# A hybrid decoder layer on one core: 16 more tokens by gathered expert rows, a dense stage on 336 instead of 352, and other queues and pacing

## Chip, core and metric

The kernel runs on one core of a Trainium2 chip. The metric is the device time of one execution in microseconds; the kernel before was timed three times. One execution was also profiled; the numbers below are from it.

## The reference

For 512 tokens of width 2048 the layer does two things, in fp32:

```
h = rms_norm(x);  proj = h @ w_in
y_a = causal attention, 16 latent heads (q, k, v from low-rank projections, rotary part)
y_b = causal attention, 16 heads with forget gates
x  = x + (concat(y_a, y_b) * sigmoid(gates)) @ w_out            # out projection, 4096 x 2048
h2 = rms_norm(x);  q = h2 @ w_q                                 # 8 heads x 2 x 128
s1, s2 = q . sub_keys (128 keys each); top 16 of each; the 256 sums; top 16 of these
e  = i1 * 128 + i2 (of 16384 experts);  g = softmax of the 16 scores
out = x + sum over the 128 picks of a token: g * gelu(h2 . u[e]) * v[e]
```

Each token so picks 8 heads x 16 = 128 experts, and each expert has a row of 2048 floats (8 KB) in u and one in v.

## The kernel before

All large products are done as three fp32r matmuls on a high and a low part of each operand (`mm3`, L131). Every weight arrives in pieces of 128 x 1024 floats (512 KB, `load`, L94, on SP's queue), which are cut in two *halves*; for each half ACT casts a high part (`half_hi`, L105) and DVE subtracts it for the low part (`half_lo`, L110). Raw pieces rotate through 3 buffers, and 2 (in the output projection) or 1 (in the dense stage) spare ones from `spare` (L602), which lie in memory that an earlier phase has used.

The order of each engine's work is set at build time: a planner simulates the program and puts each engine's instructions in the order in which it finds them ready; each engine and each queue then works in that order. Pools hand out buffers, and a new tile waits for the last reader of what lay there.

**Phase 1** (0 to about 1476 us) does the projections and attention of all heads. Each head's gated output is written to `mrg` in memory (L315, on SP).

**Phase 2** (to 1924 us) is the output projection. `out0_units` (L679) does tokens 0 to 127 first, so that their experts are known early: `bring(q)` loads the merged heads of those tokens in four blocks (three on SP, one on POOL) and splits them, then 96 *early* halves (blocks 0 to 2) and 32 *late* ones (block 3) follow. The 128 *main* units (L575, `out_units`) do tokens 128 to 511 with 9 matmuls of 512 columns a half; they read `merged_half` (L631), four loads of 192 KB on ACT's queue. Six main units stand between the norm of tokens 0 to 127 and their query, 8 among the query's halves, the others after it. `select` (L793) then gives the picks of tokens 0 to 127 in `idx`.

From there on the *gathers* run beside the matmuls. One gather (`gather`, L911) is an indirect DMA on POOL that brings, for one pick of 128 tokens, 128 rows of 8 KB (1.05 MB) into one of three row buffers `rows`, and one DVE operation on 128 x 2048 floats: a dot product with h2 for u (L927), a multiply-add for v (L940). `half_lo` adds `rate` to a credit for each half and issues a gather for each whole credit (L112). In phase 2 the rate is `RATE` = 0.42 after a start of -`LAG` x `RATE`; in the dense stage it is what is left over `HALVES` = 948. There are `GATHERS` = 2 x (128 + 32): after the first 128 tokens, 32 further ones (`NX`) are gathered with four picks side by side: partition 32 j + t holds token t and the picks of block j. Their indices and gates are moved to that layout by small DMAs on ACT's queue (L906), `h0` is filled with four copies of their h2 (L932), and at the end a matmul with a 0/1 matrix `C_RM` adds the four blocks up (L975).

**Phase 3** (to about 2179 us) scales x to h2 for tokens 128 to 511 (L860), transposes and splits it (L867), does the query on 384 columns, top-k and select. The first r of the dense stage (`ahead`) are mixed in.

**Phase 4**, the dense stage, does the experts for the remaining TD = 384 - 32 = 352 tokens without gathering: all 16384 experts, with zero gates for those not picked. `gate_matrix` (L979) builds the gates from the picks, four tokens at a time (a *group*: 3 + 1 DVE compares, 3 ACT scalings, 4 matmuls, one ACT copy). `up_stream` (L1026) computes u . h2 for 128 experts (one r) in 48 matmuls, `gated` (L1067) applies gelu and gate, and `down` (L1079) adds v's part in 48 matmuls per r. All of these have TD columns. `store` (L1100) transposes the sums back, adds x and writes.

Of the kernel before, what the change touches and what calls it, by code (L numbers as in the profile page):

```python
# [48 lines left out]
C_N = C_I2 + NKEY  # L49
# [3 lines left out]
NX = 32  # L53
NG = P // NX
# [11 lines left out]
RATE = 0.42  # L66
# [4 lines left out]
FIRST_W = {0: (0, 0), 2: (1, 0), 4: (0, 1), 6: (1, 1)}  # L71
WAIT = 6
# [6 lines left out]
class Kern:  # L79
    def __init__(self, tc, a):  # L80
        self.tc, self.nc, self.a = tc, tc.nc, a
        self.gathered, self.credit, self.rate = 0, 0.0, 0.0
        self.early = {}
        self.nraw, self.nbuf = -1, NRAW
# [182 lines left out]
    def attention(self, parts, fpart, v, gate, hx, yq=None):  # L267
# [47 lines left out]
        nc.sync.dma_start(self.mrg[hx % HEADS * 2 + hx // HEADS], gate)  # L315
# [241 lines left out]
    def phase2(self, res, sm):  # L557
# [12 lines left out]
        with self.pool(name="mgr", bufs=2) as self.mgr, self.pool(name="msp", bufs=3) as self.msp, \  # L570
# [6 lines left out]
            seq = self.out0_units(tk) + [norm] + main[:WAIT] + turns  # L577
            done = WAIT
# [16 lines left out]
            self.run(main[done:])  # L595
            self.rate = 0.0

# [33 lines left out]
    def merged_half(self, q, i):  # L631
# [47 lines left out]
    def out0_units(self, tk):  # L679
# [5 lines left out]
        def bring(q):  # L685
# [3 lines left out]
            eng = nc.gpsimd if q == 3 else nc.sync  # L689
            eng.dma_start(raw, self.mrg[q * 8:q * 8 + 8, :, 0:P].rearrange("h p t -> p h t"))  # L690
# [16 lines left out]
        def own():  # L707
# [134 lines left out]
    def phase3(self, hp):  # L842
# [7 lines left out]
        with self.pool(name="tk", bufs=2) as tk, \  # L850
# [55 lines left out]
            for j in range(NG):  # L906
                js, rows = slice(j * NX, j * NX + NX), slice(j * NX, j * NX + NX)
                nc.scalar.dma_start(self.idxx[rows], self.idx1[:NX, js])
                nc.scalar.dma_start(self.gx[rows], flat(self.gt[:, 0])[:, js])

    def gather(self, g):  # L911
        n = PH * TOPK
        if g < n:
            self.gather_u(g)
        elif g < 2 * n:
            self.gather_v(g - n)
        elif g < 2 * n + NX:
            self.extra_u(g - 2 * n)
        else:
            self.extra_v(g - 2 * n - NX)  # L920

    def gather_u(self, k):
        nc = self.nc
        row = self.rows[:, k % 3]
# [4 lines left out]
        if k == PH * TOPK - 1:  # L929
            nc.scalar.activation(self.aa, self.aa, AF.Gelu)  # L930
            nc.vector.tensor_tensor(out=self.aa, in0=self.aa, in1=self.gt0.rearrange("p a b -> p (a b)"), op=OP.mult)
            for j in range(NG):  # L932
                nc.gpsimd.dma_start(self.h0[j * NX:j * NX + NX], self.hx)

    def gather_v(self, k):
        nc = self.nc
        row = self.rows[:, k % 3]
# [7 lines left out]
    def extra_rows(self, src, s):  # L945
        row = self.rows[:, s % 3]
# [4 lines left out]
    def extra_u(self, s):  # L951
        nc = self.nc
        row = self.extra_rows("u", s)
        nc.vector.tensor_tensor_reduce(out=row, in0=row, in1=self.h0, scale=1.0, scalar=0.0,
                                       op0=OP.mult, op1=OP.add, accum_out=self.ax[:, s:s + 1])
        if s == NX - 1:
            nc.scalar.activation(self.ax, self.ax, AF.Gelu)
            nc.vector.tensor_tensor(out=self.ax, in0=self.ax, in1=self.gx, op=OP.mult)

    def extra_v(self, s):  # L960
        nc = self.nc
        row = self.extra_rows("v", s)
        sum_ = self.h0
        if s == 0:
            nc.vector.tensor_scalar(out=sum_, in0=row, scalar1=self.ax[:, 0:1], scalar2=None, op0=OP.mult)
        else:
            nc.vector.scalar_tensor_tensor(out=sum_, in0=row, scalar=self.ax[:, s:s + 1], in1=sum_,
                                           op0=OP.mult, op1=OP.add)
        if s == NX - 1:
            x = self.rows[:NX, (s + 1) % 3]  # L970
# [286 lines left out]
```

## Time and profile before

| | us |
|---|---|
| three runs, median (lowest, highest) | 4208.79 (4203.27, 4209.16) |
| the profiled execution | 4210.52 |
| its span, first to last instruction | 4208.7 |

| engine | busy us | share of the span |
|---|---|---|
| PE (matmul) | 4107.9 | 98% |
| PEld (weight load, beside PE) | 3716.1 | 88% |
| DVE | 3094.0 | 74% |
| ACT | 1919.4 | 46% |
| POOL | 593.0 | 14% |

Matmuls are pipelined, so the mean duration of one is longer than the distance from one to the next (its pitch); a pitch is read from the count of records in a stretch that PE fills. Engine names: PE TensorE, DVE VectorE, ACT ScalarE, POOL GpSimd, SP SyncE; a q behind a name is the engine's sequencer, which waits and issues DMAs. L12 is line 12 of the kernel. In a window's row the columns are the stretch, its length, then the busy time with the number of records for PE, PEld, DVE, ACT and POOL, the granted TensorE clock as a share of 2.4 GHz, the busy share of the 16 DMA engines, and GB/s. In a timeline's row they are the start, the time from the first start to the last end of the merged instructions, engine, line, operation, out<-in, form and count, and in brackets the idle time before with what ended it.

### The profile page before, as it was taken

To read this page: it belongs to the slowest core of one execution; us is meant where nothing else is said; L and a number is where in the kernel's file an instruction comes from. 1 tells how busy PE (TensorE), PEld (TensorE's weight loads), DVE (VectorE), ACT (ScalarE), POOL (GpSimd) and SP (SyncE) were. 2 spreads that over 40 slices of the span, in tenths; PEclk is the share of its full clock that TensorE was granted. 3 is DMA by queue.
4 is the path that set the end of the run, shared out by engine and by line. 5 is a ranking of instruction groups with operands and counts; after the bars stand their busy time and mean duration, and the time that the engine had idled before them with its cause. 6 is when DMAs were issued, how large, how long until landed. Compare 5 with 4: busy or idle time off the path is not lost.

```text
span 4208.7 us, 61121 instructions
## 1 busy us (share of the span) xinstructions
PE 4107.9 (98%) x22599; PEld 3716.1 (88%) x22599; DVE 3094.0 (74%) x5344; ACT 1919.4 (46%) x3708; POOL 593.0 (14%) x487
## 2 busy tenths in 40 slices
PE   8999999999999979998999999999999999999998
PEld 6878888888888757787999999999999999999998
DVE  8555555655565678887999887777777877777775
ACT  4555545555554566333369333333333333333332
POOL 1111101111111100021001111111211221211120
PEclk9999999999999989998999999999999999999999
DMA  3222222222222388797347988888888888888885
GB/s 133 88 74 83 80 81 83 83 74 88 85 76 83 117 288 269 268 346 267 111 136 225 339 300 312 308 308 318 312 305 300 318 303 314 317 311 308 297 302 195
DMA packets 246860, 905.20 MB, mean 215 GB/s; under 512 B 22977, under 2 KB 75201, under 8 KB 202049
## 3 DMA queue, kind: packets, MB, share of 16 engines
q1 hardware_dynamic: 192208, 547.82, 38.0%
q0 software_dynamic: 46704, 339.24, 21.8%
q10 hardware_dynamic: 7648, 14.25, 1.1%
q8 instruction: 177, 2.90, 0.3%
q14 instruction: 123, 1.00, 0.1%
HBM read 862.12 MB, written 39.06 MB: 214 GB/s over the span
## 4 chain that ended last, share of the span: by engine, by line
PE 44%; ACT 3%; DMA 1%; DVE 1%; issue 1%; POOL 0%; DVEq 0%; POOLq 0%; ACTq 0%
PE acc L136 8%; PE acc L135 8%; PE acc L134 8%; PE a L136 7%; PE a L135 7%; PE a L134 7%; ACT o L1005 2%; ACT rows L1019 1%; ACT whi L105 0%; DMA rows<-v,eidx 0%; DVE wlo L110 0%; DMA rows<-u,eidx 0%; DVE rows L927 0%; PE acc L1110 0%; PE acc L975 0%
## 5 line engine op out<-in xcount | busy, mean ns | idle before, releaser
L105 ACT CAST whi<-raw 128x512 fp32r<-128x512 f32 x1820 | 1120.9, 622 | 1835.6 <-PE acc L135 679.1
L110 DVE TENSOR_TENSOR wlo<-raw,whi 128x512 fp32r<-128x512 f32 x1820 | 1230.2, 688 | 642.6 <-ACT whi L105 615.7
L135 PE MATMUL acc<-Wl,whi 128*128 128x352 f32 x2048 | 660.7, 323 | 3.5 <-DVE Wl L92 3.5
L134 PE MATMUL acc<-Wh,whi 128*128 128x352 f32 x2048 | 655.7, 323 | 0.5 <-ACT Wh L91 0.5
L134 PE MATMUL a<-dh,whi 128*128 128x352 f32 x1984 | 640.7, 323 | 0.0
L135 PE MATMUL a<-dl,whi 128*128 128x352 f32 x1984 | 638.8, 322 | 0.0
L136 PE MATMUL a<-dh,wlo 128*128 128x352 f32 x1984 | 634.2, 322 | 1.7 <-DVE wlo L110 1.6
L136 PE MATMUL acc<-Wh,wlo 128*128 128x352 f32 x2048 | 627.0, 323 | 1.9 <-DVE wlo L110 1.9
L134 PE MATMUL mm<-hh,whi 128*128 128x512 f32 x1424 | 572.5, 402 | 8.3 <-ACT hh L536 8.3
L135 PE MATMUL mm<-hl,whi 128*128 128x512 f32 x1424 | 571.6, 402 | 6.2 <-DVE hl L537 6.0
L136 PE MATMUL mm<-hh,wlo 128*128 128x512 f32 x1424 | 569.8, 400 | 0.0
L135 PEld LDWEIGHTS acc<-Wl,whi 128*128 128x128 f32 x2048 | 385.4, 188 | 4.1 <-DVE Wl L92 4.1
L134 PEld LDWEIGHTS acc<-Wh,whi 128*128 128x128 f32 x2048 | 384.0, 188 | 1.8 <-issue 0.8
L136 PEld LDWEIGHTS acc<-Wh,wlo 128*128 128x128 f32 x2048 | 379.3, 188 | 3.1 <-DVE wlo L110 3.1
L136 PEld LDWEIGHTS a<-dh,wlo 128*128 128x128 f32 x1984 | 371.3, 188 | 2.9 <-DVE wlo L110 2.7
L135 PEld LDWEIGHTS a<-dl,whi 128*128 128x128 f32 x1984 | 372.4, 188 | 0.0
L134 PEld LDWEIGHTS a<-dh,whi 128*128 128x128 f32 x1984 | 372.4, 188 | 0.0
L135 PEld LDWEIGHTS mm<-hl,whi 128*128 128x128 f32 x1424 | 269.5, 189 | 72.3 <-DVE hl L537 11.1
L134 PEld LDWEIGHTS mm<-hh,whi 128*128 128x128 f32 x1424 | 270.2, 190 | 68.9 <-ACT hh L536 8.3
L136 PEld LDWEIGHTS mm<-hh,wlo 128*128 128x128 f32 x1424 | 269.6, 189 | 61.0 <-issue 0.2
L940 DVE SCALAR_TENSOR_TENSOR x<-rows,aa,x 128x2048 f32<-128x2048 f32 x128 | 300.1, 2345 | 2.2 <-DMA rows<-v,eidx 2.2
L927 DVE CUSTOM_DVE_ANT_0 rows<-rows,h 128x2048 f32<-128x2048 f32 x128 | 292.3, 2284 | 8.7 <-DMA rows<-u,eidx 8.7
(383 smaller groups left out, 6050.2 us busy)
## 6 DMA issues: line engine op xcount, KB each, us to landing
raw<-ut SPq DMA_DIRECT2D x256, 512.0 KB, 5.1
raw<-vt SPq DMA_DIRECT2D x256, 512.0 KB, 5.7
raw<-w_in SPq DMA_DIRECT2D x178, 512.0 KB, 3.7
raw<-w_out SPq DMA_DIRECT2D x128, 512.0 KB, 5.2
raw<-w_pq SPq DMA_DIRECT2D x64, 512.0 KB, 4.0
gd<-rows SPq DMA_DIRECT2D x22, 1024.0 KB, 5.8
G<-gd SPq DMA_DIRECT2D x15, 1408.0 KB, 8.0
raw<-w_up SPq DMA_DIRECT2D x24, 512.0 KB, 3.6
```

What stands on the lines that cost most here:

```text
L105: self.nc.scalar.copy(hi, src)
L110: ins = self.nc.vector.tensor_tensor(out=lo, in0=src, in1=hi.bitcast(F32), op=OP.subtract)
L134: nc.tensor.matmul(out, wh, xh, start=start, stop=False)
L135: nc.tensor.matmul(out, wh, xl, start=False, stop=False)
L136: nc.tensor.matmul(out, wl, xh, start=False, stop=stop)
L927: nc.vector.tensor_tensor_reduce(out=row, in0=row, in1=self.h0, scale=1.0, scalar=0.0, op0=OP.mult, op1=OP.add, accum_out=self.aa[:, k:k + 1])
L940: nc.vector.scalar_tensor_tensor(out=self.x1[0], in0=row, scalar=self.aa[:, k:k + 1], in1=self.x1[0], op0=OP.mult, op1=OP.add)
L1005: nc.scalar.activation(o1[:, i], o1[:, i], AF.Copy, scale=lists[:, 2, t0 + i:t0 + i + 1])
L1019: nc.scalar.copy(st[:, :, t4:t4 + 4], ps.rearrange("p t i -> p i t"))
```

## The change

- **Tokens.** 16 further tokens (`GROUPS` = (0, 32), (32, 16)) are gathered, with eight picks side by side. `NX` becomes 48, TD 336, `GATHERS` 352. The second group runs behind the first, with its own spread of h2 (8 copies), its own columns of indices and gates, and a 0/1 matrix `C_RB` for its reduction. The first group's sum now goes to `x1[0]`, whose store is done, so that `h0` is free for the second spread. Row buffers rotate by one counter (`next_row`).
- **Pacing.** `RATE` 0.46; the last `REST` = 10 main units of phase 2 give no credit.
- **Queues.** The gated output of the last two heads (hx 15 and 31) is written from POOL. All four `bring` loads go on POOL, the first three before any unit. `merged_half` loads its four heads by one DMA of 768 KB on SP into one buffer, behind a one-element DVE copy that waits for the last low part made (`load_after`), and splits two heads at a time.
- **Order.** `merged_half(0, 0)` comes after 64 early halves, `merged_half(0, 1)` after the first 8 late ones; `FEW` = 4 main units stand among the late halves, one behind each 8.
- **Buffers.** `w` in the dense stage, which `store` uses too, has four buffers instead of two.

```diff
+GROUPS = ((0, 32), (32, 16))
+NX = sum(n for _, n in GROUPS)
-RATE = 0.42
+RATE = 0.46
+REST = 10
+FEW = 4
@@ attention
-        nc.sync.dma_start(self.mrg[hx % HEADS * 2 + hx // HEADS], gate)
+        eng = nc.gpsimd if hx % HEADS == HEADS - 1 else nc.sync
+        eng.dma_start(self.mrg[hx % HEADS * 2 + hx // HEADS], gate)
@@ phase2
-            seq = self.out0_units(tk) + [norm] + main[:WAIT] + turns
-            done = WAIT
+            seq = self.out0_units(tk, main) + [norm] + main[FEW:FEW + WAIT] + turns
+            done = FEW + WAIT
...
-            self.run(main[done:])
+            self.run(main[done:-REST])
             self.rate = 0.0
+            self.run(main[-REST:])
@@ merged_half
-        for j in range(4):
-            m = self.mgr.tile([P, n], F32, name="m")
-            nc.scalar.dma_start(m, self.mrg[8 * q + 4 * i + j, :, t0:])
-            self.split(mh[:, j], ml[:, j], m)
+        m = self.mgr.tile([P, 4, n], F32, name="m")
+        k = 8 * q + 4 * i
+        self.load_after(m, self.mrg[k:k + 4, :, t0:].rearrange("h p t -> p h t"))
+        for j in (0, 2):
+            self.split(mh[:, j:j + 2], ml[:, j:j + 2], m[:, j:j + 2])
@@ out0_units
-            eng = nc.gpsimd if q == 3 else nc.sync
-            eng.dma_start(raw, self.mrg[q * 8:q * 8 + 8, :, 0:P].rearrange("h p t -> p h t"))
+            nc.gpsimd.dma_start(raw, self.mrg[q * 8:q * 8 + 8, :, 0:P].rearrange("h p t -> p h t"))
...
-        out = [self.bare(bring, q) for q in range(3)] + early[:48] + [self.bare(own)] + early[48:] + [self.bare(bring, 3)]
-        return out + late[:12] + [self.bare(self.merged_half, 0, 0)] + late[12:24] + \
-            [self.bare(self.merged_half, 0, 1)] + late[24:]
+        for q in range(3):
+            bring(q)
+        half = lambda i: [self.bare(self.merged_half, 0, i)]
+        out = early[:40] + [self.bare(own)] + early[40:64] + half(0) + early[64:] + [self.bare(bring, 3)]
+        for i in range(0, len(late), 8):
+            out += late[i:i + 8] + main[i // 8:i // 8 + 1] + (half(1) if i == 8 else [])
+        return out
@@ phase3
-            for j in range(NG):
-                js, rows = slice(j * NX, j * NX + NX), slice(j * NX, j * NX + NX)
-                nc.scalar.dma_start(self.idxx[rows], self.idx1[:NX, js])
-                nc.scalar.dma_start(self.gx[rows], flat(self.gt[:, 0])[:, js])
+            for o, n in GROUPS:
+                m = P * n // P
+                for j in range(P // n):
+                    js, rows = slice(j * m, j * m + m), slice(j * n, j * n + n)
+                    nc.scalar.dma_start(self.idxx[rows, o:o + m], self.idx1[o:o + n, js])
+                    nc.scalar.dma_start(self.gx[rows, o:o + m], flat(self.gt[:, 0])[o:o + n, js])
@@ gather
+    def spread(self, i):
+        o, n = GROUPS[i]
+        for j in range(P // n):
+            self.nc.gpsimd.dma_start(self.h0[j * n:j * n + n], self.hx[o:o + n])
+
+    def next_row(self):
+        self.nrow += 1
+        return self.rows[:, self.nrow % 3]
...
-        sum_ = self.h0
+        sum_ = self.x1[0] if i == 0 else self.h0
...
+            pick = C_RM if n == 32 else C_RB
             for c in range(4):
...
+                nc.tensor.matmul(ps[:n], self.cst[:, pick:pick + n], sum_[:, cs], start=True, stop=True)
@@ gated, store
-        w = self.wp.tile([P, 512], F32, name="w", bufs=2)[:, :TD]
+        w = self.wp.tile([P, 512], F32, name="w", bufs=4)[:, :TD]
```

## Rows read from the trace of the kernel before

**Rows 1.** The page: busy time by engine; the chain by engine.

```profile
PE 4107.9 (98%) x22599; PEld 3716.1 (88%) x22599; DVE 3094.0 (74%) x5344; ACT 1919.4 (46%) x3708; POOL 593.0 (14%) x487
...
PE 44%; ACT 3%; DMA 1%; DVE 1%; issue 1%; POOL 0%; DVEq 0%; POOLq 0%; ACTq 0%
```

**Rows 2.** Windows: stretch, length, PE PEld DVE ACT POOL busy (records), clock, DMA, GB/s.

```profile
1480.00:1620.00 140.00, 120.10 (x473) 87.23 (x474) 102.94 (x166) 90.94 (x164) 0.93 (x1) 0.93 0.84 288
1760.00:1780.00 20.00, 20.00 (x88) 16.16 (x87) 16.23 (x21) 6.22 (x10) 3.61 (x4) 1.00 1.00 402
1760.00:1900.00 140.00, 140.00 (x607) 113.36 (x606) 122.72 (x159) 49.63 (x91) 28.29 (x27) 1.00 0.93 353
1924.00:2000.00 76.00, 56.10 (x291) 51.83 (x291) 57.84 (x109) 23.18 (x49) 8.18 (x9) 0.82 0.67 258
2180.00:2310.00 130.00, 128.74 (x948) 123.62 (x947) 127.10 (x277) 130.00 (x372) 16.61 (x23) 1.00 0.74 210
2340.00:4140.00 1800.00, 1797.36 (x11216) 1795.62 (x11215) 1423.70 (x1803) 671.65 (x1174) 330.92 (x275) 1.00 0.85 309
```

**Rows 3.** Waits of PE: total us, times, longest.

```profile
PE pa L134 <- ACT whi L105: 12.7, 2, 12.5
PE tp L866 <- DVE dl L92: 12.5, 4, 7.0
```

**Rows 4.** Windows filled by matmuls of 256, of 352 and of 384 columns.

```profile
168.00:172.50 4.50, 4.50 (x39) 4.50 (x38) 3.14 (x6) 4.11 (x8) 0.00 (x0) 1.00 0.04 15
3000.00:3100.00 100.00, 100.00 (x625) 100.00 (x624) 79.47 (x93) 36.29 (x62) 20.03 (x15) 1.00 0.84 309
2001.00:2028.00 27.00, 27.00 (x157) 27.00 (x157) 26.97 (x134) 9.58 (x17) 0.00 (x0) 1.00 0.42 121
```

**Rows 5.** Groups by form, PE, one product of three: count, busy, mean ns, idle.

```profile
L134 PE MATMUL acc<-Wh,whi 128*128 128x352 f32 x2048 | 655.7, 323 | 0.5 <-ACT Wh L91 0.5
L134 PE MATMUL a<-dh,whi 128*128 128x352 f32 x1984 | 640.7, 323 | 0.0
...
L134 PE MATMUL acc<-dh,whi 128*128 128x352 f32 x64 | 20.8, 326 | 0.5 <-ACT whi L105 0.5
```

**Rows 6.** Timeline of DVE at the second border.

```profile
1932.49 2.29 DVE L927 CUSTOM_DVE_ANT_0 rows<-rows,h 128x2048 f32<-128x2048 f32 x1 [1.16 <-DMA rows<-u,eidx]
...
1938.22 2.29 DVE L927 CUSTOM_DVE_ANT_0 rows<-rows,h 128x2048 f32<-128x2048 f32 x1 [3.43 <-DMA rows<-u,eidx]
...
1979.10 2.28 DVE L927 CUSTOM_DVE_ANT_0 rows<-rows,h 128x2048 f32<-128x2048 f32 x1
```

**Rows 7.** The reduction's matmuls; the timeline of the tail.

```profile
L975 PE MATMUL acc<-h,cst x8: 593/593/617, 4144.6 to 4147.6; 128*32 128x512 f32 x8
...
4198.47 1.28 DVE L1111 TENSOR_TENSOR w<-w,acc 128x512 f32<-128x512 f32 x2 [0.57 <-PE acc L1110]
...
4201.71 0.33 ACTq L1107 DMA_DIRECT2D w<-xs  x1
4204.69 0.69 DVE L1111 TENSOR_TENSOR w<-w,acc 96x512 f32<-96x512 f32 x1 [4.93 <-DMA w<-xs]
```

**Rows 8.** Two lines' instructions: duration ns min/median/max, first and last start us.

```profile
L1018 PE MATMUL acc<-o,o x704: 270/275/378, 2179.1 to 2308.7; 128*128 128x128 f32 x176
...
L908 ACTq DMA_DIRECT2D idxx<-idx x4: 514/558/1432, 2172.4 to 2175.2; - x4
```

**Rows 9.** Timelines of ACT and of SP at the first border.

```profile
1484.98 0.51 ACT L91 CAST mh<-m 128x384 fp32r<-128x384 f32 x1 [6.18 <-DMA m<-mrg]
...
1459.20 17.63 SPq L315 DMA_DIRECT2D mrg<-gate  x2
...
1479.04 19.66 SPq L98 DMA_DIRECT2D raw<-w_out  x7
```

**Rows 10.** DMA issues: count, KB each, median us to landing.

```profile
raw<-mrg SPq DMA_DIRECT2D x3, 512.0 KB, 4.1
...
raw<-mrg POOLq DMA_DIRECT2D x1, 512.0 KB, 7.7
```

More of the change, by code (lines that the diff above doesn't have):

```diff
@@ L81, in __init__ @@
         self.tc, self.nc, self.a = tc, tc.nc, a
-        self.gathered, self.credit, self.rate = 0, 0.0, 0.0
+        self.gathered, self.credit, self.rate, self.nrow = 0, 0.0, 0.0, -1
         self.early = {}
@@ L569, in phase2 @@
         self.ss = sm.tile([P, NT, 4], F32, name="ss")
[L570 removed]
+        with self.pool(name="mgr", bufs=1) as self.mgr, self.pool(name="msp", bufs=3) as self.msp, \
                 self.pool(name="tka", bufs=1) as tk, self.spare(NRAW2, NSP2), \
@@ L677, in bare, with out0_units @@
         return lambda: None, lambda w: f(*v)
-    def out0_units(self, tk):
+    def out0_units(self, tk, main):
         nc, a = self.nc, self.a
@@ L916, in gather @@
             self.gather_v(g - n)
-        elif g < 2 * n + NX:
-            self.extra_u(g - 2 * n)
-        else:
-            self.extra_v(g - 2 * n - NX)
+        else:
+            g -= 2 * n
+            for i, (o, m) in enumerate(GROUPS):
+                if g < m:
+                    return self.extra_u(i, o, m, g)
+                if g < 2 * m:
+                    return self.extra_v(i, o, m, g - m)
+                g -= 2 * m
+    def spread(self, i):
[5 more added lines that the diff above has]
+        return self.rows[:, self.nrow % 3]
     def gather_u(self, k):
         nc = self.nc
-        row = self.rows[:, k % 3]
+        row = self.next_row()
         nc.gpsimd.indirect_dma_start(out=row, out_offset=None, in_=self.a["u"],
@@ L931, in gather_u @@
             nc.vector.tensor_tensor(out=self.aa, in0=self.aa, in1=self.gt0.rearrange("p a b -> p (a b)"), op=OP.mult)
-            for j in range(NG):
-                nc.gpsimd.dma_start(self.h0[j * NX:j * NX + NX], self.hx)
+            self.spread(0)
     def gather_v(self, k):
         nc = self.nc
-        row = self.rows[:, k % 3]
+        row = self.next_row()
         nc.gpsimd.indirect_dma_start(out=row, out_offset=None, in_=self.a["v"],
@@ L945, in extra_rows @@
     def extra_rows(self, src, s):
-        row = self.rows[:, s % 3]
+        row = self.next_row()
         self.nc.gpsimd.indirect_dma_start(out=row, out_offset=None, in_=self.a[src],
@@ L974, in extra_v @@
                 ps = self.acc.tile([P, 512], F32, name="acc")
-                nc.tensor.matmul(ps[:NX], self.cst[:, C_RM:C_RM + NX], sum_[:, cs], start=True, stop=True)
-                nc.vector.tensor_tensor(out=x[:, cs], in0=x[:, cs], in1=ps[:NX], op=OP.add)
-            nc.sync.dma_start(self.a["out"][P:P + NX], x)
+                nc.tensor.matmul(ps[:n], self.cst[:, pick:pick + n], sum_[:, cs], start=True, stop=True)
+                nc.vector.tensor_tensor(out=x[:, cs], in0=x[:, cs], in1=ps[:n], op=OP.add)
+            nc.sync.dma_start(self.a["out"][P + o:P + o + n], x)
     def gate_matrix(self, pool, acc, ahead):
@@ L1105, in store @@
             n = min(P, TD - q)
-            x = self.wp.tile([P, 512], F32, name="w", bufs=2)[:n]
+            x = self.wp.tile([P, 512], F32, name="w", bufs=4)[:n]
             nc.scalar.dma_start(x, self.xs[NX + q:NX + q + n, cs])
@@ L1179, in constants @@
         c[:, C_RM + h] = (p % 32 == h)
+    for h in range(16):
+        c[:, C_RB + h] = (p % 16 == h)
     c[:, C_IF] = (np.float32(10000.0) ** (-np.arange(32, dtype=np.float32) / np.float32(32)))[p % 32]
```

36 lines of the change are left out of this document (19 added, 17 removed).

## Prediction, made before the result was known

> **What bounds the kernel now.** I read the page's busy line and chain first, then busy time by stage, matmul pitch by width, TensorE's waits, and last the timelines at the stage borders. TensorE is busy 98% of the span and holds 44% of the chain; no other engine has more than 3% [rows 1]. By stage this is sharper: from 2340 to 4140 us, the dense expert stage, PE is busy 1797.4 of 1800 us at full granted clock with 11216 matmuls, while DMA moves 309 GB/s at share 0.85 and DVE is busy 79% [rows 2]. Nothing but the number of matmuls and the pitch of one sets that stage. What PE loses lies at the borders: 20 of 140 us from 1480 to 1620 at a mean clock of 0.93, and 20 of 76 us from 1924 to 2000 at 0.82 [rows 2]; its two largest waits are there, 12.7 us on a weight cast and 12.5 us on a split of the transposed h2 [rows 3].
>
> **The dense columns.** A matmul takes the time of its columns plus a constant: 100/625 = 160 ns at 352 columns, 27/157 = 172 ns at 384 and 4.5/38 = 118 ns at 256 [rows 4]; at 512 it is 140/607 = 231 ns [rows 2]. (A window counts a record at its edges, so the short ones are good to 3%.) The slopes are 0.38, 0.44 and 0.44 ns a column, so 16 columns fewer save 6.0 to 7.1 ns; I take 6.8, on the side of the longer windows. Three products each of 2048, 1984 and 64 matmuls run at this width [rows 5]: 12288 x 6.8 ns = 84 us (74 to 87). All of it is on the path, since PE has no other limit there; what is late next is a transfer or DVE, below.
>
> **The 32 more gathers.** Pacing gives 114 x 0.42 - 4.2 = 43 gathers in the output projection now and leaves 277 for the 948 halves of the dense stage, 0.292 a half. After: 100 x 0.46 - 4.6 = 41, and 311 left, 0.328 a half. A half is 12 matmuls, so the window holds 11216/12 = 935 halves and gets 34 more gathers: 35 MB at 1.05 MB each, and 34 x 2.3 us = 78 us of DVE [rows 6]. At the new pitch its 11216 matmuls take 11216 x 153.7 ns = 1724 us. DVE: (1424 + 78)/1724 = 87%; DMA: (556 + 35) MB/1724 us = 343 GB/s. The nearest row is the output projection, 1760 to 1900 us: 353 GB/s, DVE 122.7 of 140 us (88%), PE 140.00 of 140; for 20 us even 402 GB/s [rows 2]. So both loads have been carried beside a full PE, but for 140 us, not for 1700. Lower bound 0; upper, the rival below; I take +5 us for late landings, about twice the 2.6 us that PE idles in the stage today. The second group's reduction adds 4 fp32 matmuls, 8 records on PE: now 8 from 4144.6 to 4147.6 us [rows 7], so +3.5 us. The extra spreads of h and the row rotation hang on POOL, which is busy 331 of 1800 us [rows 2], and cost nothing unless a gather waits behind them: the second spread is issued 32 gathers before its use.
>
> **Gate matrix and index moves.** 88 groups become 84. The groups run from 2179.1 to 2308.7 us [rows 8], 1.47 us each, ACT 130.00 of 130 us busy [rows 2]: -5.9 us. Ahead of it ACT issues 12 index copies instead of 4, 0.56 us each [rows 8]: +4.5 us on the engine that is the limit. The 8 more gate copies are spread over the four query columns, where ACT is under half busy (49.6 of 140 us in the projection before it [rows 2]); 0. Net -1.5 us (-6 to +5).
>
> **First border, mixers to output projection.** PE stands until 1488.2 us for the first cast. ACT, in order, sat 6.18 us before a merged-heads piece until 1484.98, then cast the third block and only then the weights; SP sat behind the last gate's write for 17.63 us from 1459.2 and sent the next weight only at 1479.04 [rows 9]. Afterwards the merged halves can't come early (their load waits for a DVE copy behind a late weight), and the gate's write and the three blocks are POOL's. So both stalls go. Next late is the last gate itself: the two spare raw buffers lie where its tile lay (the 1479.04 load waited for that write), and the first weights now fall to them. With the write at about 1480, 4.5 us of flight and 0.6 us of cast I get 1485.5: -2.5 us. The four early main halves bring 9 matmuls of 231 ns each against some 0.9 us of DMA, and give back about 1.2 us each of the DMA-bound stretch: -5 us. Against it, 1.5 MB of merged heads leave the idle stretch for that one: 1.5 MB at 288 GB/s = +5 us. Sum -3 us. Ends: all 12.7 us and the slow clock gone with the halves' gain, -18; the brings late on POOL and the first weights with them, +10. A block took 7.7 us to land from POOL against 4.1 from SP [rows 10], which is hidden if the blocks go out as soon as hT's room and the raw buffers are free, some 20 us ahead of 1476.
> The Trainium skill (DMA: Bandwidth & Descriptors, Issuing engines are not separate DMA queues) says that DMAs from any engine share the same 16 DMA engines, so that another issuer saves only issue time. By that rule the moves would bring 0 in place of -3, and the sum below would be 3 us higher; the 17.63 us above were a wait in SP's order, which the rule doesn't price.
>
> **Second border.** After the last projection matmul DVE waits 1.16 and 3.43 us for two gathered rows, each followed by 2.29 us of work, before it splits the first h2; eight more such 2.28 us operations follow, the last at 1979.10 [rows 6]. Stopping the credits 10 halves (21 us) earlier and 41 instead of 43 should leave fewer behind. But the gathers don't run at the credit: 27 in 140 us [rows 2], one in 5.2 us or 2.5 halves, is 0.40 a half; the three row buffers hold them back. A higher rate doesn't help that, so I count two gathers fewer at 2.3 us: -4 us (-20 if none is left behind, +4 if one more is).
>
> **Tail.** With two w buffers the last 96 rows' x is asked for at 4201.71, after a store has landed, and added at 4204.69; the other two adds end by 4199.75 [rows 7]. With four it is loaded before: the add follows at once, -5 us (-4 to -7).
>
> **Sum.** -84 + 5 + 3.5 - 1.5 - 3 - 4 - 5 = -89 us. The profiled execution took 4210.5 us (span 4208.7 and 1.8 around it), 1.7 above the median of 4208.79; 4121.5, or **4120** against the median.
>
> **Rivals.**
> *The DMA engines become the bound, and it gets slower.* Place: the dense stage. It must move 591 MB in the window. The terms outside it sum to -10 us, so it breaks even if the window takes 1810 us, 327 GB/s; if no more than today's 309 can be sustained, 1913 us, 113 longer: 4210 + 113 - 10 = 4313 us. For it: share 0.85 already and four raw buffers only. Against it: 353 GB/s for 140 us beside a full PE [rows 2]. 5%; that it holds 327 to 340 and eats part of the gain (4140 to 4200), 6%.
> *Weight loads set the pitch, not columns.* PEld is busy 1795.6 of 1800 us in the dense stage, and 113.4 of 140 in the projection [rows 2]. Then 16 columns save nothing, and the time is 4210.5 + 3.5 - 13.5 + 5 = 4205. Against it: at 256 columns, the same 128x128 load, PEld is just as full (4.50 of 4.50 us) at 118 ns, and at 384 the pitch is longer than at 352 [rows 4]. 2%.
> The Trainium skill (Perfetto Trace Analysis, Identifying the Most-Contended Engine) takes the busy share of LDWEIGHTS as a good measure of how near TensorE is to its limit; read so, the dense stage is full by its loads and this rival is right. By that rule the sum would be 4205, by the pitch rows 4120.
> *Both borders clear.* If the stalls of [rows 3] go with their slow clock, -18 and -20 stand in place of -3 and -4: 4089 us. For it: both stalls have one plain cause each [rows 6, 9]. Against it: the spare buffers and the three row buffers, above. 7%.
>
> **Chances.** My forecast, 80%, has its own range of 4100 to 4140. Same means within 0.2% (8.4 us), about what a measurement of this kernel can tell from no change. Faster: 80 + 6 + 7 = 93%; same: 2%; slower: 5%. The range that should hold 8 in 10, with the partial DMA case and most of the cleared borders, is 4090 to 4160.
>
> **What would show it.** In the dense stage, 100 us should hold about 650 matmuls (625 now) at some 343 GB/s, share near 0.94, DVE 87%, PE above 99%. The matmul groups should read 336 columns and their mean fall by about 7 ns. If PE waits for casts that wait for ut or vt loads, or DVE sits before gathered rows, the DMA rival is at work. The gate matrix's records should be 672 instead of 704. At the first border the largest PE wait should be under 12 us, with no ACT idle on merged heads; at the second fewer than ten gather operations should follow the h2 scale; the last add should directly follow the other two. I am wrong if the pitch in a full stretch stays near 160 ns, or if PE idles over 20 us in the dense stage.

## The result, and the profile after

Four runs of the changed kernel took 4158.22 us in the median (4153.74 to 4159.76), four of the kernel before beside them 4208.98 (4203.27 to 4210.86). The ratio is 0.9882, with a 95% interval of 0.9869 to 0.9894: 51 us faster, where 89 were forecast. The profiled execution took 4157.29 us (span 4155.5), against 4121.5 in the sum. So 35.8 us are to be explained.

The page of the kernel after answers to [rows 1]: PE is busy less of the span than before (97 against 98%), and its share of the chain has fallen from 44 to 37%.

```profile
PE 4035.3 (97%) x22575; PEld 3633.3 (87%) x22575; DVE 3138.3 (76%) x5377; ACT 1899.2 (46%) x3677; POOL 642.0 (15%) x531
...
PE 37%; issue 5%; ACT 2%; DVE 1%; POOL 1%; DMA 1%; DVEq 0%; POOLq 0%; ACTq 0%
```

The windows of the kernel after, with the columns of [rows 2] and [rows 4]:

```profile
1480.00:1620.00 140.00, 124.11 (x482) 90.10 (x482) 102.61 (x168) 89.53 (x161) 0.91 (x1) 0.95 0.84 293
1760.00:1900.00 140.00, 138.10 (x596) 111.33 (x596) 116.63 (x151) 47.44 (x81) 32.68 (x26) 1.00 0.91 349
1924.00:2000.00 76.00, 56.96 (x301) 51.66 (x300) 59.51 (x95) 24.04 (x50) 9.74 (x10) 0.87 0.74 276
2180.00:2310.00 130.00, 125.56 (x926) 121.19 (x927) 124.72 (x273) 127.69 (x368) 16.90 (x22) 0.97 0.71 203
2340.00:4090.00 1750.00, 1737.02 (x11224) 1726.04 (x11223) 1482.28 (x1859) 660.87 (x1175) 374.90 (x317) 1.00 0.90 338
2800.00:3000.00 200.00, 200.00 (x1302) 199.79 (x1301) 169.91 (x202) 78.52 (x140) 47.68 (x39) 1.00 0.92 341
```

The last row gives the pitch: 200/1302 = 153.6 ns against 160 [rows 4]. The row above it gives the loss. 11224 matmuls of 153.6 ns are 1724 us, and the window is 1750: 26 us went, of which the busy time shows only half (1750 - 1737 = 13). The other half is matmuls that started late without PE being counted idle. In the dense stage before, 11216 x 160 = 1795 of 1800 us [rows 2]: 5 us.

By stage, from the starts of the first and last matmul of each in the two traces:

| stage, us | before | after | change |
|---|---|---|---|
| to the last attention matmul | 1475.3 | 1471.6 | -3.7 |
| to the first peer query matmul of tokens 128 to 511 (output projection) | 457.1 | 467.4 | +10.3 |
| peer query, first to last matmul (second border) | 176.5 | 171.7 | -4.8 |
| to the first gate matmul | 70.1 | 73.4 | +3.3 |
| gate matrix, to the first down product | 137.4 | 131.8 | -5.6 |
| first to last matmul of the down products (dense stage) | 1880.5 | 1832.2 | -48.3 |
| to the end | 11.7 | 7.4 | -4.3 |

The fifth row counts from the first gate matmul, the sixth holds 11616 matmuls in both kernels.

Waits of PE, and last one of ACT, in the trace after (total us, times, longest):

```profile
PE acc L139 <- DVE wlo L113: 15.9, 17, 3.9
PE pa L137 <- ACT whi L108: 12.4, 4, 10.5
PE tp L875 <- DVE dl L95: 11.6, 3, 6.9
PE acc L1013 <- ACT lists L1015: 5.1, 1, 5.1
...
ACT whi L108 <- DMA raw<-vt: 59.5, 25, 5.4
```

and two of the same waits in the trace before:

```profile
ACT whi L105 <- DMA raw<-vt: 13.6, 6, 4.5
...
PE acc L136 <- DVE wlo L110: 6.5, 6, 3.9
```

The two largest of [rows 3] are still there, a little smaller. New at the top is PE waiting for the low part of a weight, and ACT now waits 59.5 us for weights of the down product (`raw<-vt`). The prediction named as the sign of the DMA rival: "if PE waits for casts that wait for ut or vt loads". Its second half is there; PE itself waits for low parts. The experiments had to say whether the late loads are the cause.

Not all of the waits for low parts lie in the dense stage. From 2340 to 4090 us they are, before and after:

```profile
PE acc L136 <- DVE wlo L110: 1.9, 3, 0.7
```

```profile
PE acc L139 <- DVE wlo L113: 11.0, 13, 1.8
```

One such stall on DVE of the kernel after (timeline, columns as in [rows 6]):

```profile
3861.76 0.50 DVE L1123 TENSOR_TENSOR x<-x,acc 128x336 f32<-128x336 f32 x1 [2.94 <-PE acc L139]
3862.18 0.68 DVE L113 TENSOR_TENSOR wlo<-raw,whi 128x512 fp32r<-128x512 f32 x1
3862.78 0.50 DVE L1123 TENSOR_TENSOR x<-x,acc 128x336 f32<-128x336 f32 x1
3863.19 1.29 DVE L113 TENSOR_TENSOR wlo<-raw,whi 128x512 fp32r<-128x512 f32 x2
3864.40 2.34 DVE L994 SCALAR_TENSOR_TENSOR x<-rows,ax,x 128x2048 f32<-128x2048 f32 x1
```

and PE at the same place:

```profile
3864.53 0.57 PE L139 MATMUL acc<-Wh,wlo 128*128 128x336 f32 x2 [1.74 <-DVE wlo L113]
3867.40 0.58 PE L139 MATMUL acc<-Wh,wlo 128*128 128x336 f32 x2 [0.72 <-DVE wlo L113]
```

DVE sat 2.94 us before an add. That add takes up the finished sums of a pair of outputs, so it waits for PE's last matmul of the pair. Splits that PE needs for the next pair stand behind it, so PE stops, then a 2.34 us gather operation goes ahead of the next split, and PE stops again.

### The profile page after: what moved, and what is told of

The parts are those of the page before. It is cut to its first block, busy times and chain, and to the rows that moved or that the text cites. A ratio compares the mean times of both kernels' runs of the same rounds, so it can differ in the third digit from the quotient of the medians.

```text
span 4155.5 us, 61144 instructions
## 1 busy us (share of the span) xinstructions
PE 4035.3 (97%) x22575; PEld 3633.3 (87%) x22575; DVE 3138.3 (76%) x5377; ACT 1899.2 (46%) x3677; POOL 642.0 (15%) x531
## 5 line engine op out<-in xcount | busy, mean ns | idle before, releaser
L137 PE MATMUL acc<-Wh,whi 128*128 128x336 f32 x2048 | 642.2, 317 | 7.3 <-DVE x L1121 4.6
L138 PE MATMUL acc<-Wl,whi 128*128 128x336 f32 x2048 | 644.4, 316 | 0.0
L137 PE MATMUL a<-dh,whi 128*128 128x336 f32 x1984 | 629.2, 317 | 0.8 <-ACT whi L108 0.8
L138 PE MATMUL a<-dl,whi 128*128 128x336 f32 x1984 | 626.5, 316 | 0.0
L139 PE MATMUL a<-dh,wlo 128*128 128x336 f32 x1984 | 621.2, 316 | 0.9 <-DVE wlo L113 0.9
L139 PE MATMUL acc<-Wh,wlo 128*128 128x336 f32 x2048 | 607.7, 318 | 11.5 <-DVE wlo L113 11.0
L137 PEld LDWEIGHTS acc<-Wh,whi 128*128 128x128 f32 x2048 | 384.8, 188 | 10.5 <-issue 6.6
L139 PEld LDWEIGHTS acc<-Wh,wlo 128*128 128x128 f32 x2048 | 375.7, 188 | 17.7 <-DVE wlo L113 17.5
L138 PEld LDWEIGHTS mm<-hl,whi 128*128 128x128 f32 x1424 | 268.6, 189 | 73.5 <-DVE hl L541 11.7
```

Source lines behind the costliest of these rows:

```text
L137: nc.tensor.matmul(out, wh, xh, start=start, stop=False)
L138: nc.tensor.matmul(out, wh, xl, start=False, stop=False)
L139: nc.tensor.matmul(out, wl, xh, start=False, stop=stop)
```

## The experiments

All times are medians with the ratio to runs of the kernel before on the same chip. The changed kernel's ratio is 0.9882 with some 0.0013 (5 us) to either side, so a total within 5 us of 4158 tells nothing, and where a stage answers the question the stage is quoted.

### The two parts of the change (e1_tokens, e2_order)

```diff
e1_tokens, from the changed kernel: RATE 0.42, no REST, no FEW, out0_units and
merged_half of the kernel before, gates written on SP, w with 2 buffers
e2_order, from the changed kernel:
-GROUPS = ((0, 32), (32, 16))
+GROUPS = ((0, 32),)
-name="w", bufs=4
+name="w", bufs=3
```

> The kernel before with the 16 further tokens alone (336 dense tokens, two groups of side tokens); queues, pacing, order of the output projection and the two w buffers as before. Theory 1 (the stage ledger of the two traces): the changed kernel is 53 us faster because the token part gives 50 (48 from the first down product to the last, 5 in the gate matrix, -3 ahead of it), while the queue part gives 4 at the mixers' end, 5 at the second border and 4 in the tail and costs 10 in the output projection. Then this kernel takes about 4159 us (4153 to 4164), its output projection ends near 1924 us as before, and its dense stage idles as in the changed kernel. Theory 2 (the queue part caused the stalls of the dense stage, since a rate of 0.46 and the early stop shift gathers): the stalls go, about 20 us less, near 4139.

> The changed kernel with one group of 32 side tokens, so 352 dense tokens: queues, pacing and order alone. Three w buffers stand in for four, since four don't fit beside 352 columns. Theory 1 (the ledger): -4 at the mixers' end, +10 in the output projection, -5 at the second border, -2 to -4 in the tail: 4205 us (4200 to 4209), ratio 0.998 to 1.0. Theory 2 (the 10 us lost in the output projection are not of the new order but came with the tokens): 4195, ratio 0.9965.

The tokens alone: 4161.58 us, 0.9887 (0.987 to 0.9903). The queues alone: 4206.49 us, 0.9997 (0.9987 to 1.0007). In the first, output projection and peer query take 453.1 and 174.5 us, and the dense stage 1832.3, as in the changed kernel. In the second they take 461.2, 171.8 and 1879.6 us. So theory 1 holds twice: the whole gain is the tokens', the queue part nets nothing, and the dense stage's loss came with the 336 columns, not with the pacing.

### Transfers against arithmetic (e3_half_transfers, e4_half_arith)

```diff
e3_half_transfers, in gather_u (in gather_v and extra_rows without `k < 64 or`)
+        if k < 64 or k % 2 == 0:
             nc.gpsimd.indirect_dma_start(out=row, ...)
e4_half_arith, in gather_u (at the other three places without `k < 64 or`, for v without the memset)
+        if k < 64 or k % 2 == 0:
             nc.vector.tensor_tensor_reduce(out=row, ...)
+        else:
+            nc.vector.memset(self.aa[:, k:k + 1], 0.0)
```

> The changed kernel, with every second gather's transfer left out from the 64th pick on (the vector operation works on what the row buffer holds; the gathered tokens' sums are wrong by that). Theory DMA (the 20 us that the dense stage lost beyond the pitch are late weight loads, 338 GB/s at share 0.90): about 150 MB less, some 255 GB/s, no load late, 4158 - 20 = 4138 (4132 to 4143), and PE's waits for splits in the down product nearly gone. Theory DVE (splits stand in VectorE's order behind an add that waits for PE and behind a 2.3 us gather operation): the same operations are left, so at most 5 us go: 4153 to 4158.

> The changed kernel, with every second gather's vector operation left out from the 64th pick on (a one-column memset in its place, or nothing), all transfers kept. Theory DVE: VectorE falls from 85 to some 67% of the dense stage, the 2.3 us ahead of late splits are gone in half of the cases and the queue catches up between: at least 14 of the 20 us go, 4138 to 4144. Theory DMA: the same megabytes, so at most 5 us go: 4153 to 4158.

Half the transfers: 4142.48 us, 0.9835 (0.9819 to 0.9851), dense stage 1825.5 us. Half the arithmetic: 4154.33 us, 0.987 (0.9853 to 0.9886), dense stage 1831.6 us. The dense stage of the first:

```profile
2340.00:4070.00 1730.00, 1721.53 (x11139) 1715.35 (x11138) 1469.73 (x1844) 664.44 (x1166) 223.84 (x173) 1.00 0.72 253
```

and of the second:

```profile
2340.00:4070.00 1730.00, 1714.96 (x11078) 1704.78 (x11077) 1169.87 (x1691) 648.41 (x1158) 328.03 (x316) 1.00 0.89 338
```

A DVE busy 68% of the time (1169.87/1730) loses as much as one busy 85%. So DVE's load is not the cause, and my second theory fell as it was put. Only 7 us came back in the stage with half the transfers, though the DMA engines were then at 253 GB/s, where the kernel before moved 309 beside a full PE [rows 2]. (The profiled execution is 9.7 us shorter than the changed kernel's; 4.0 of it are in the projection, where nothing was edited.)

The 7 us are less than the transfers are worth, though. The edit begins behind the 64th gather, at some 2433 us, and from 2460 to 3800 us the changed kernel (first row) and this one (second) compare so:

```profile
2460.00:3800.00 1340.00, 1333.18 (x8629) 1327.43 (x8627) 1134.01 (x1412) 508.45 (x903) 289.04 (x248) 1.00 0.91 340
2460.00:3800.00 1340.00, 1338.74 (x8692) 1337.39 (x8691) 1141.73 (x1419) 520.23 (x911) 171.73 (x130) 1.00 0.72 249
```

Here 63 matmuls more went through, 63 x 153.6 ns = 9.7 us, which is two thirds of what the changed kernel lost in this stretch (1340 us hold 8724 at the pitch, 95 more than it did). Behind it, at 3919 us, PE waited 4.1 us again, for a split behind a gather operation that had waited 4.57 us for its row. So the first theory is not refuted by this run. What the run leaves open is how fewer transfers help: by loads that land in time, or by the order of DVE's queue, which the planner makes anew in each kernel.

### The order of adds and splits, and a fifth buffer (e5_adds, e6_raw5)

```diff
e5_adds, in down()
                 w = self.weight(self.a["vt"][c, dp, u])
+                if pend:
+                    with self.tc.issue_after(self.split_ins):
+                        pend.pop()()
...
+            if last or dp == 7:
+                adds()
+            else:
+                pend.append(adds)
e6_raw5, in phase4()
-            with self.spare(1):
+            with self.spare(2):
```

> The changed kernel with one order fixed: in the down product the two adds of a finished pair of outputs are queued on VectorE behind the first two weight splits of the next pair (they stood ahead of them in places, waiting for PE's last matmul). Theory order (PE's 22 us beyond the pitch in the dense stage come from the order that the planner gave VectorE, add before split): at least 10 of them go, first to last down product 1832 to about 1820 us, total near 4147. Theory loads (the splits are late because their weights land late, the order only shows it): at most 3 go, 4154 to 4160.

> The changed kernel with a fifth raw weight buffer in the dense stage (and two more split buffers' share of it unchanged). Theory bursts (338 GB/s can be sustained, and single loads are late because gathers of 1 MB and gate slices of 1.3 MB go ahead of them while only four buffers of 3.7 us each cover that): casts' waits for vt loads, 60 us now, fall by more than half and 8 to 14 us go, about 4146. Theory bandwidth (the engines are at their limit): one more buffer is filled once and then empty, at most 3 us go, 4154 to 4160.

The adds behind the next two splits: 4134.01 us, 0.9826 (0.981 to 0.9842), dense stage 1811.9, 20.3 us less. (e11_three below has the same order in this stage and took 1817.0, so 15 to 20 us.) Up to the first down product its engines' orders are those of the changed kernel, so the rest of its 24 us is no effect of the edit. Its dense window:

```profile
2340.00:4070.00 1730.00, 1726.49 (x11202) 1722.01 (x11201) 1482.63 (x1858) 656.22 (x1173) 369.59 (x317) 1.00 0.91 341
```

its waits for vt loads, and from 2340 to 4090 us those for low parts:

```profile
ACT whi L108 <- DMA raw<-vt: 62.5, 26, 4.1
```

```profile
PE acc L139 <- DVE wlo L113: 1.0, 2, 0.7
```

and the same window of the changed kernel:

```profile
2340.00:4070.00 1730.00, 1717.02 (x11094) 1706.04 (x11093) 1466.43 (x1839) 652.47 (x1160) 372.81 (x316) 1.00 0.90 338
```

The casts still wait for vt loads, 62.5 us against 59.5, at a slightly higher rate (341 against 338 GB/s), and PE hardly notices: 108 matmuls more in the window, and 1.0 us of waits for splits, in 2 places, where there were 11.0 in 13. In the stretch from 2460 to 3800 us, where half the transfers gave 63 matmuls, the order gives 72, with all transfers:

```profile
2460.00:3800.00 1340.00, 1339.48 (x8701) 1338.55 (x8700) 1145.03 (x1421) 511.73 (x916) 290.50 (x250) 1.00 0.91 343
```

DVE itself waits for PE in front of adds as long as it did (61.3 us in this kernel, 56.6 in the changed one, 25.0 before); only what stands behind the adds is another. The late loads were real and, in this order, harmless; what cost was the add in front of the split. Theory order held.

The fifth buffer: 4145.84 us, 0.9857 (0.9841 to 0.9873), dense stage 1823.1, 9 us less. The casts' waits for vt loads fell from 59.5 to 18.4 us, as the theory of bursts has it, and most of PE's waits for splits stayed (13.5 us in the whole trace against 15.9). But the 9 us lie elsewhere. The start of the stage in the changed kernel and in this one, and this one's long window:

```profile
2316.00:2340.00 24.00, 17.24 (x105) 16.72 (x104) 16.92 (x27) 7.67 (x16) 4.15 (x4) 0.94 1.00 390
```

```profile
2316.00:2340.00 24.00, 23.74 (x155) 23.46 (x154) 17.86 (x28) 7.45 (x13) 5.39 (x5) 1.00 1.01 403
2340.00:4070.00 1730.00, 1719.36 (x11096) 1709.76 (x11096) 1473.63 (x1841) 656.30 (x1165) 387.54 (x317) 1.00 0.91 339
```

The first 24 us hold 50 matmuls more, 7.7 us; the 1730 us behind them hold 11096 where the changed kernel has 11094. In the changed kernel the largest loss at the start is one wait of PE, 4.6 us, for a copy on DVE behind a gather operation that had waited 4.50 us for its row, and not for a weight. So with two thirds of the loads' lateness gone, nothing came back in the long stretch where the loads had been late, and the theory of bursts got its number by luck. A new planner's order comes with every edit, so I can't say how much of the 9 us is the buffer itself.

### Issue place and loads of the queue part (e7_halves, e8_idx)

```diff
e7_halves, in merged_half
-        self.load_after(m, self.mrg[k:k + 4, :, t0:]...)
+        self.nc.sync.dma_start(m, self.mrg[k:k + 4, :, t0:]...)
e8_idx, in phase3
-                    nc.scalar.dma_start(self.idxx[rows, o:o + m], ...)
+                    nc.gpsimd.dma_start(self.idxx[rows, o:o + m], ...)
```

> The changed kernel, with the merged halves' loads no longer tied behind a VectorE copy, so that SP can issue the first ones while PE still stands between mixers and projection. Theory A (the output projection takes 453 to 459 us in the new order against 445 to 449 in the old one because 1.5 MB of merged heads moved out of the idle stretch into the DMA-bound one): some 5 us come back, about 449 us from the last attention matmul to the last projection matmul, 4153. Theory B (the loss is in the order of the pieces or in the blocks brought by POOL): it stays at 453 to 459 and the total at 4158.

> The changed kernel with the 12 index copies issued by POOL and not by ACT. Theory (as in the prediction's term): they hold ACT, and with it the list copies that the gate matrix waits for, 5.1 us of PE idle at 2177: from the last query matmul to the first gate matmul 73 us become 68, total 4153. Rival (POOL's issues are slower and the transposes wait for something else that is then late): 73 us stay, 4158.

Early halves: 4143.73 us, 0.9846 (0.983 to 0.9863). Theory A is wrong for its own stage: the projection stayed at 464.3 us. Of the 13.6 us between the two profiled executions, the largest part is at the second border, where the peer query took 165.1 us instead of 171.7. The planner left fewer gather operations among the splits of h2 there (seven behind the first h2 scale, nine in the changed kernel, ten before), which I had not foreseen; that this is the reason is argued. 3.1 us are in the projection, the rest is spread.

Index copies on POOL: 4148.54 us, 0.9861 (0.9845 to 0.9877), and 67.0 us from the last query matmul to the first gate matmul, where the changed kernel has 73.4 and the eight others with 48 gathered tokens and the copies on ACT 72.2 to 74.9. ACT of the kernel after, at that place:

```profile
2176.36 5.64 ACTq L919 DMA_DIRECT2D idxx<-idx  x9
2182.04 1.69 ACT L1015 COPY lists<-acc 128x80 f32<-128x80 f32 x8 [5.24 <-DMA idxx<-idx]
```

and with the copies on POOL:

```profile
2174.14 0.51 ACT L1015 COPY lists<-acc 128x80 f32<-128x80 f32 x3
...
2176.24 0.96 ACT L1015 COPY lists<-acc 128x128 f32<-128x128 f32 x5
```

Nine issues of 0.6 us stood in ACT's order ahead of copies that were ready, and PE waited 5.1 us for them (the fourth wait above). Theory confirmed.

### The first border (e9_first, e10_main)

```diff
e9_first, in out0_units
         for q in range(3):
             bring(q)
+        self.nraw += 2
e10_main
-FEW = 4
+FEW = 0
-            out += late[i:i + 8] + main[i // 8:i // 8 + 1] + ...
+            out += late[i:i + 8] + ...
```

> The changed kernel, with the two raw buffers that lie where the last gate's tile lay skipped once, so that the first projection weights fall to buffers that are free at 1452 us. Theory (as in the prediction's step for the first border: next late is the last gate itself, since its room holds the first weights): the first casts are done before the last attention matmul and PE's 10.9 us there shrink to 2 to 4, and since the stretch behind it is bound by DMA about half of that is given back: 4152 to 4155. Rival (the first blocks of merged heads, brought by POOL, or PE's clock set the gap): 10 us stay, 4158.

> The changed kernel with the four early main pieces taken back out of the first 128 pieces. The output projection takes about 8 us longer in the new order than in the old (463 against 455 us from the last attention matmul to the first peer query matmul, over nine traces). Theory (the early pieces cost, since each needs three split pairs of merged heads before it and a place among the raw buffers): it falls to 455, total 4150. Rival (as predicted, they give back 1.2 us each of a DMA-bound stretch, and the loss is in the merged halves and the blocks brought by POOL): it grows to 467, total 4162.

In the changed kernel ACT waits for the weight that fell to the gate's room; the gate's write goes out at 1473.07 on POOL, the weight behind it at 1475.52 on SP:

```profile
1481.82 1.14 ACT L108 CAST whi<-raw 128x512 fp32r<-128x512 f32 x2 [10.63 <-DMA raw<-w_out]
...
1473.07 0.54 POOL L319 DMA_DIRECT2D mrg<-gate  x1 [11.63 <-DVE gate L317]
...
1475.52 0.80 SPq L101 DMA_DIRECT2D raw<-w_out  x2
```

With the skip (4139.59 us, 0.9848, 0.9831 to 0.9866) the first projection matmuls run from 1458.0 us, 18 of them ahead of the last attention matmul, but the gap stays at 9.6 us, since the fourth weight falls to the same room. 18 x 0.231 = 4.2 us; the projection takes 458.6 us against 459.1 to 467.4 in the six traces of this order with 48 gathered tokens and no edit there. So the gate's room is what held the first weights, as the prediction had it, but the gap itself did not shrink to 2 to 4 us: another weight is late behind the same write. The rest of the gain lies again at the second border (162.4 us) and in the dense stage (1824.5, 7.7 us less), where nothing was meant.

Without the early main pieces: 4146.7 us, 0.9857 (0.9841 to 0.9874), projection 459.6 us. The total is 11.5 us under the changed kernel's, more than the 5 us that tell nothing, and the rival's 4162 did not come. But the projection is at the lower edge of the same 459.1 to 467.4, so that the early pieces cost is likely and not shown by the stage.

### Together (e11_three, e12_all)

```diff
e11_three = e5_adds + e7_halves + e8_idx
e12_all = e5_adds + e8_idx +
-REST = 10
+REST = 40
@@ load
+        if self.hold and self.nraw % self.nbuf >= NRAW:
+            self.hold, self.nraw = self.hold - 1, self.nraw + self.nbuf - NRAW
@@ out0_units
+        self.hold = 3
```

> The changed kernel with three of the edits together: adds behind the next splits in the down product (alone 24 us under the changed kernel), merged halves loaded early (alone 14), index copies on POOL (alone 10). If each works at its own place they add up: by the stage times 20 in the dense stage, 6 ahead of the gate matrix, 7 to 10 at the second border, so 4121 to 4126 us. Rival: PE's idle time is given back by late loads in the dense stage, since the stage now moves more per us (share 0.91 already): 4134 as with the adds alone.

> The changed kernel with what the runs so far point to: adds behind the next splits in the down product, index copies on POOL, the first nine projection weights kept to the three raw buffers that are free early (the skip of the run before, three times), and the gathers' credits stopped 40 halves and not 10 before the end of the projection. Expected by stage against the changed kernel: dense stage -17 to -20, ahead of the gate matrix -6; first border and projection -4 to -8 (one skip gave 4 us there, as 18 matmuls moved ahead of the gap); second border -8 to -15, as no gather operation then stands between the splits of h2 (171.7 us for the peer query stage should become 157 to 164). Sum -35 to -49: 4109 to 4123 us, with 4115 the likeliest. Rival: the 16 gathers more in the dense stage than in the changed kernel (DMA share over 0.91) take 10 us back there: 4125.

The three edits together: 4122.8 us, 0.9801 (0.9784 to 0.9817), inside the range expected from their sum. It is the fastest measured, 35 us under the changed kernel. Its terms differ from the expected ones: the dense stage at 1817.0 us gives 15 of 20, the 69.2 us ahead of the gate matrix 4 of 6, and the peer query at 160.5 us 11 where 7 to 10 were expected.

The last one missed: 4132.38 us, 0.9817 (0.9804 to 0.9831). Two of its steps did what they should: the peer query takes 157.1 us, and the gap at the first border is gone, 0.3 us between the last attention and the next projection matmul. But attention now ends at 1477.5 us, 6 later, and the projection takes 471.5 us, with new gaps inside. ACT served projection weights ahead of the attention that everything waits for: its last copy for the attention comes at 1476.88, behind casts that had waited for a weight and for PE. The stretch behind was no faster:

```profile
1480.00:1620.00 140.00, 118.20 (x450) 85.22 (x448) 94.55 (x156) 80.11 (x147) 1.26 (x2) 0.93 0.84 286
```

286 GB/s at share 0.84, about as in the changed kernel and before [rows 2], with fewer matmuls. In the dense stage, which 14 gathers more were left for, the rival's size came true: 1824.3 us, 12 more than with the adds alone, at

```profile
2340.00:4070.00 1730.00, 1724.13 (x11165) 1718.98 (x11164) 1508.58 (x1874) 650.02 (x1169) 372.63 (x330) 1.00 0.92 348
```

and here, in one place, a load is what PE waits for: a cast for a vt load, and at the same time PE for the cast:

```profile
2888.63 1.14 ACT L110 CAST whi<-raw 128x512 fp32r<-128x512 f32 x2 [2.63 <-DMA raw<-vt]
```

```profile
2889.30 0.65 PE L139 MATMUL acc<-Wh,whi 128*128 128x336 f32 x1 [4.36 <-ACT whi L110]
```

(This kernel's lines stand two further down.) From 2340 to 4090 us PE waits 4.9 us for casts, in 2 places; another 4.5 us, at 2326, stand behind a gathered row that came late. So the cause of the 12 us is shown in part only, and no limit between 341 and 348 GB/s is shown either. The kernel e11_three has e5_adds' order through the whole dense stage, moved the same 341 GB/s, took 5 us longer there and had one wait for a cast too, of 1.9 us; and 353 GB/s passed beside a full PE for 140 us [rows 2].

## Why the prediction was right in direction and 36 us short

The sign and the mechanism of the gain (fewer columns a matmul) were right. The median lies inside the stated range of 4090 to 4160, 2 us below its upper end, and that is partly luck: the partial DMA rival had been taken into the range, and the time got there another way. The forecast's own range of 4100 to 4140 was not met. The 35.8 us by terms:

| term | predicted | measured | missed by |
|---|---|---|---|
| dense columns | -84 | 12288 x 6.4 ns = -78.6 | 5.4 |
| late landings and the second reduction | +8.5 | 11616 x 6.4 = 74.3 due, 48.3 got: +26 | 17.5 |
| first border with the projection | -3 | -3.7 + 10.3 = +6.6 | 9.6 |
| gate matrix and index moves | -1.5 | +3.3 - 5.6 = -2.3; 672 dense matmuls lie there, 672 x 6.4 ns = -4.3, so +2 without them | 3.5 |
| second border | -4 | -4.8 | -0.8 |
| tail | -5 | -4.3 | 0.7 |

**Dense columns.** Right in kind; 6.4 ns where 6.8 was taken. The slope from 352 down to 336 is 0.40 ns a column, the lower end of 0.38 to 0.44 [rows 4] was nearer. The rival that weight loads set the pitch is refuted: PEld is as full as before (199.79 of 200 us), and the pitch fell. The Trainium skill (Perfetto Trace Analysis, Identifying the Most-Contended Engine) takes the busy share of LDWEIGHTS, beside MFU, as a measure of how near TensorE is to its limit; here it read full at 160 and at 153.6 ns alike, so the measurement decides against that reading.

**Late landings.** This is the step that failed: "Lower bound 0; upper, the rival below; I take +5 us". The time came out where the partial DMA rival had it (4140 to 4200, at 6%), with 338 GB/s inside its 327 to 340. Its mechanism did not: with the adds moved behind the splits, the loads are as late, the rate is higher, and 20.3 of the 26 us are back (some 3.5 of the 26 are the second reduction, which was right). What the transfers did, they did together with the order: half of them left out helped too, in the stretch where they were out. I had asked only which engine would run out of time or bandwidth, and counted DVE's 87% (85% came) as harmless. An engine that works in order can stop PE at 85% and, in e4_half_arith, at 68%, when it waits for PE itself with PE's next input queued behind. The kernel before had the same order in places, at a cost of 1.9 us in the dense stage, so it could have been seen: DVE waits for PE in front of adds there too, 25.0 us in all. That the planner left fewer splits ahead of the adds at 336 columns can be counted in the traces: DVE had split at least four later halves ahead of a pair's first add in 115 of 128 pairs before and in 77 in the changed kernel; with half the transfers it is 112, with five buffers 99. That fits a planner that finds loads late in its own simulation, but why it does so was not tried: this is argued, not shown.

**First border.** PE's largest wait there is 10.5 us (under 12, as said), no ACT idle on merged heads is left, and the first cast comes at 1481.8 for the reason given: the last gate's room. But of the 2.5 us expected there and the 5 that the early main halves should give back nothing arrived; the projection took some 8 us longer than in the old order (a median of 463.1 in seven traces, against 457.1 and 453.1 in only two). Not the time of the merged halves (e7_halves), and not the first casts (e9_first). The step that failed is the 5 us of the early main halves or the price of what moved there: e10_main, without them, was faster in total. Whether the 8 us are the blocks on POOL, the earlier place of x and the gains (2 MB), or partly the early main pieces is open. In e12_all the gap closed and the projection ended later: the stretch behind ran at 286 GB/s, as it did at 288 to 293 in the other two. That its transfers set it, so that time won ahead of it is given back there, fits this and is not shown, since at share 0.84 the DMA engines are not full and move 349 GB/s later in the same projection. The prediction used that rule for the halves ("DMA-bound stretch") and did not apply it to the gap itself.

**Index moves.** The 4.5 us were right (5.1 us of PE idle). On moving work between issuers, the Trainium skill (DMA: Bandwidth & Descriptors, Issuing engines are not separate DMA queues) says that only issue time is saved. e8_idx agrees, 6.4 us for 12 issues of 0.5 to 0.6. The queue part as a whole, ratio 0.9997, fits too but is no test of it, since its terms have both signs.

**Second border and tail.** Nine gather operations instead of ten after the h2 scale, where two fewer were counted on at 2.3 us each: the -4.8 us came out near the -4 partly by luck. In the tail the last adds follow each other without a wait, where [rows 7] shows 4.93 us:

```profile
4149.48 1.88 DVE L1138 TENSOR_TENSOR w<-w,acc 128x512 f32<-128x512 f32 x3 [0.50 <-PE acc L1137]
```

**The signs I gave.** 651 matmuls in 100 us, 338 GB/s at share 0.90 (343 and 0.94 were expected), DVE 85%, PE 99.3% busy, 672 gate records: all near. "PE idles over 20 us" was a bad sign to watch: by busy time it idled 13 us, by count and pitch it lost 26.

## What to carry to other kernels

When a change shortens the engine that sets the time, look first in the order of the in-order engines beside it: an instruction that waits for that engine, with that engine's next input queued behind, costs little while enough of that input is ready (1.9 us of PE's waits in the dense stage before) and a lot once it is not (15 to 20 us here). Read the loss as records times pitch against the window, not as idle time, and read an experiment in the stretch where its edit acts. And before paying for a gap ahead of a stretch with its own limit, make sure that the stretch can use the time.

## What the runs showed that was not expected

- At 341 GB/s and share 0.91 over 1730 us the DMA engines served a PE that was busy 1726.49 us.
- Waits of casts for loads of 62.5 us in total cost PE next to nothing; 11.0 us of its own waits for splits in the dense stage came with 26 us lost.
- The changed kernel, e3_half_transfers, e5_adds and e8_idx have the same instructions in the same order in the output projection and took 467.4, 463.4, 460.7 and 467.3 us for it in their profiled executions. The same order so moves by some 7 us from one execution to the next, as much as the edits there. In the dense stage e5_adds and e11_three, of one order, are 5 us apart.
